# Sixteen row sets change products, three queues change hands, and two gate units change places in a transformer block

## The chip, the cores and the metric

One Trainium2 chip, of which the kernel uses one core. The metric is the device time of one execution in microseconds; the kernel before took 3376.22 us (median of 3 runs, 3374.99 to 3377.64).

A core has five engines with queues of their own: TensorE (PE, with its weight loads as PEld), VectorE (DVE), ScalarE (ACT), GpSimd (POOL) and SyncE (SP). Each works its queue in order. Transfers are issued from the queues of SP, ACT and POOL and share 16 DMA engines.

## The reference, cut to what matters

All tensors are 4-byte floats; there are 512 tokens of width 2048.

```python
h   = rmsnorm(x);  q, k, v, z, gate = split(h @ w_in)
o_a = differential attention of q, k, v (8 heads, chunk mask), normed per head
o_b = spatial gating of gelu(z)
x   = x + (sig(g_A) * (o_a @ P_A) + sig(g_B) * (o_b @ P_B)) @ w_out
# product-key experts ("PEER"), h = rmsnorm(x):
s   = (h @ w_q) against two lists of 128 keys       # 8 heads
16 best of each list, then the 16 best of the 256 sums -> 128 expert numbers and gates a token
a   = h . u_emb[id];  act = gelu(a) * gate;  x = x + sum(act * v_emb[id])
y   = rmsnorm(x) * final_norm
```

## The kernel before

Every dense product is made exact in three passes: a weight tile `raw` is cast to a high half `wh` on ScalarE (L847, L151), VectorE takes the low half `wl = raw - wh` (`split_low`, L111), and TensorE multiplies high by high, high by low and low by high (`mm3`, L162).

The 512 tokens are treated in three ways. The first 128 ("first block") go ahead alone through all layers. Then the other 384 pass attention, gMLP, merge and output product. For the expert layer the tokens split again: 224 tokens, the first block and two extra groups of 64 and 32 (`XG`, each spread over the 128 partitions), are done **sparsely**: GpSimd gathers 128 rows of a table at a time (`indirect_dma_start`, L302), a "set" of 1 MB. A set of `u_emb` costs VectorE one pass that forms a dot product (L281), a set of `v_emb` one pass that adds a scaled row to an accumulator (L288). The remaining 288 tokens (`TD`) are done **densely** over all 16384 experts: the first product (256 steps of 24 matmuls, two steps to a column block `pa`) gives the activations `ga`, stored to `ga_d` by ScalarE's queue (L939); meanwhile a gate matrix is built from one-hots (`gates()`, 72 builds of 4 matmuls `pgt`) and stored to `g_d` in 18 chunks of 16 tokens (L909). The second product (16 groups of 16 steps of 24 matmuls `pvt`) loads `ga` and the gates back (`load_ga`, `load_g`), multiplies them (`gated`, L961), splits the result (`split_gated`) and multiplies it with `v_tiles`; each step's result is added into `accT` by `settle` (L1044).

Sets are spread over the work by a plan. `items` lists them in order: 128 u sets of the first block, its 128 v sets, 96 u sets of the extra groups, their 96 v sets. `knots` gives how many are due at which step (the steps of the first product start at `AT_U` = 240, of the second at `AT_V` = 496), linear between knots; `sparse_step` gathers what is due now and lets VectorE use what was due `GBUF` = 4 steps earlier. 212 are due when the first product starts, and 352 (`U_END`) from 8 steps before the second. The gather waits for a recent `wl` on VectorE (`pace`).

The routing of a 128-token block (`route`) runs on VectorE in portions handed out two steps at a time (`credit`): top 16 lists, then the expert numbers by one-hot sums (L410 to L416), in 4-byte tiles `oh` and `tif`. Block 1 ends by copying numbers and gates into the slots of the extra groups, twelve small transfers on ScalarE's queue (L433, L434).

From L934 on (the first and second product) instructions stand in each queue as written. Ahead of that a scheduler orders them by the program's order and by when tiles come free. `merge` (L724) multiplies a sigmoid of a gate projection (`unit`) with a branch product; its tile pool `gt` (2 buffers) is opened after the attention pools are closed. The last head's norm (`head_norm(att, *tail)`, L716) stands ahead of it.

In the second product `load_g(grp + 2)` is one transfer of 1152 KB on ScalarE's queue at the first step of each group; the first two stand in the last 32 steps of the first product, after the gate matrix is done. At its step 20 the first block's rows are closed (`finish_rows(acc0, ...)`), and each extra group's rows are closed when its last v set is used.

Of the kernel before, what the change touches and what calls it, by code (L numbers as in the profile page):

```python
# [53 lines left out]
def hybrid_block(ctx, tc, x, attn_norm, attn_col, w_in, diff_lambda, diff_subln, gmlp_norm, gmlp_row, wsT, gmlp_bs,  # L54
# [186 lines left out]
    def turned(pair, at, src):  # L241
        for q in range(src.shape[-1] // 512):
# [14 lines left out]
    items = [(table, g, s) for groups in ([-1], range(len(XG))) for table in (u_emb, v_emb)  # L257
             for g in groups for s in range(SLOTS if g < 0 else XSETS[g])]
    U_END = 2 * SLOTS + sum(XSETS)
    AT_U, AT_V = 240, 240 + 2 * NE  # L260
    knots = [(14, 0), (AT_U, 212), (AT_V - 8, U_END), (AT_V, U_END), (AT_V + 222, len(items))]
# [108 lines left out]
    def route(rtp, gbp, tb):  # L370
# [27 lines left out]
        tif = rtp.tile([P, 2 * HEADS, TOPK], F32, name="tif")  # L398
# [5 lines left out]
        for p, rf in enumerate(at):  # L404
            sel = rtp.tile([P, HEADS, TOPK], F32, name=f"sel{p}")
            for hh_ in range(0, HEADS, 2):
                hs = slice(hh_, hh_ + 2)
                oh = rtp.tile([P, 2, TOPK, TOPK], F32, name="oh")
                ohf = oh.rearrange("p h k r -> p (h k) r")
                nc.vector.tensor_tensor(  # L410
                    ohf, rf[:, hs].rearrange("p h k -> p (h k)").unsqueeze(2).to_broadcast([P, 32, TOPK]),
                    iota_f[:, :TOPK].unsqueeze(1).to_broadcast([P, 32, TOPK]), op=OP.is_equal)
                nc.vector.tensor_tensor(
                    oh, oh, tif[:, 2 * hh_ + p:2 * hh_ + 4:2, :].unsqueeze(2).to_broadcast(
                        [P, 2, TOPK, TOPK]), op=OP.mult)
                nc.vector.tensor_reduce(sel[:, hs].rearrange("p h k -> p (h k)"), ohf, axis=AX.X, op=OP.add)  # L416
                yield 1.8
            cols.append(sel.rearrange("p h k -> p (h k)"))
# [6 lines left out]
        if tb == 1:  # L425
# [3 lines left out]
            for g, (t0, n) in enumerate(XG):  # L429
                m = XSETS[g]  # L430
                for j in range(P // n):
                    to, of = slice(j * n, (j + 1) * n), (slice(t0 - P, t0 - P + n), slice(j * m, (j + 1) * m))
                    nc.scalar.dma_start(xslot_e[g][to, :], ei[of])  # L433
                    nc.scalar.dma_start(xslot_g[g][to, :], gf[of])  # L434
# [248 lines left out]
    aa = branch_tiles(0)  # L683
    with tc.tile_pool(name="att", bufs=2, reuse_waits="tile") as att, \
            tc.tile_pool(name="att1", bufs=1, reuse_waits="tile") as att1:
        tail = None
        for h in range(HEADS):
# [27 lines left out]
            tail = (po[:, :LB, :], aa, (slice(None), h))  # L715
        head_norm(att, *tail)  # L716
# [7 lines left out]
    def merge(br, pair):  # L724
        with tc.tile_pool(name="gt", bufs=2, reuse_waits="tile") as gt:
            def unit(n):
                sg = gt.tile([P, LN], F32, name="sg")
                nc.scalar.activation(sg, project(w_in[G0 + KT * br + n], hh, "gate"), AF.Sigmoid)
                return sg

            ahead = [unit(0)]
            for n in range(KT):
                if n + 1 < KT:
                    ahead.append(unit(n + 1))
# [10 lines left out]
    merge(0, aa)  # L745
# [39 lines left out]
    merge(1, bb)  # L785
# [165 lines left out]
    def load_g(grp):  # L951
        if grp < NG:
            gms[grp] = pools["vp"].tile([P, NCH, VG, GCH], F32, name="vg", bufs=2)
            nc.scalar.dma_start(
                gms[grp], g_d[:, :, grp * VG:(grp + 1) * VG, :].rearrange("c p e t -> p c e t"))
# [23 lines left out]
    for i in range(NE):  # L979
        ps = pp_tile("pa")[:, :TD]  # L980
        for half in range(2):
# [17 lines left out]
            if "vp" not in pools and rgen is None and ggen is None:  # L999
# [3 lines left out]
                load_g(0)  # L1003
            elif "vp" in pools:
                u, odd = divmod(step - opened - 2, 2)
# [7 lines left out]
                if u == 5 and not odd:  # L1013
                    load_g(1)
# [8 lines left out]
    with tc.tile_pool(name="pv", bufs=4, space=PSUM, reuse_waits="tile") as pv_pool, \  # L1023
# [89 lines left out]
        for step in range(KT * NG):  # L1113
# [5 lines left out]
            for j in range(VG):  # L1119
# [3 lines left out]
                mm(pv, lo[:, j, :], aH, start=False, stop=j == VG - 1)  # L1123
            if w == 0:
                if n == 0:
                    load_g(grp + 2)
# [17 lines left out]
            if step == 20:  # L1144
# [90 lines left out]
```

## Time and profile before

| | us |
|---|---|
| median of 3 runs | 3376.22 |
| the profiled execution | 3376.36 |
| its span, first to last instruction | 3374.7 |
| TensorE busy | 3245.8 |
| VectorE busy | 2803.2 |
| ScalarE busy | 1561.5 |
| GpSimd busy | 681.0 |

The first product runs from about 1570 to 2518 us of the span, the second from 2518 to 3358. Busy times are sums over the whole span, and its stretches differ; a stretch has to be read by itself. The mean granted clock of TensorE is 0.987 of its full speed. Matmul records overlap, so TensorE counts as busy while its next matmul is already queued.

### The profile page before, as it was taken

To read this page: it belongs to the slowest core of one execution; us is meant where nothing else is said; L and a number is where in the kernel's file an instruction comes from. 1 tells how busy PE (TensorE), PEld (TensorE's weight loads), DVE (VectorE), ACT (ScalarE), POOL (GpSimd) and SP (SyncE) were. 2 spreads that over 40 slices of the span, in tenths; PEclk is the share of its full clock that TensorE was granted. 3 is DMA by queue.
4 is the path that set the end of the run, shared out by engine and by line. 5 is a ranking of instruction groups with operands and counts; after the bars stand their busy time and mean duration, and the time that the engine had idled before them with its cause. 6 is when DMAs were issued, how large, how long until landed. Compare 5 with 4: busy or idle time off the path is not lost. (4 is left out here: it accounts for less than half of the span.)

```text
span 3374.7 us, 53163 instructions
## 1 busy us (share of the span) xinstructions
PE 3245.8 (96%) x20545; PEld 3012.0 (89%) x20545; DVE 2803.2 (83%) x3784; ACT 1561.5 (46%) x2367; POOL 681.0 (20%) x512
## 2 busy tenths in 40 slices
PE   8999999989999999899899999999999999999997
PEld 6577588889989997799899999999999999999997
DVE  7489579888888888899899999777767999989985
ACT  6377234332233332333363588888434343343343
POOL 0000002222322224222223222222321111111100
PEclk9999999999999999899999999999999999999998
DMA  8899847769999999788889999999999999989973
GB/s 321 289 338 349 296 140 253 292 232 357 351 357 339 361 346 411 305 329 315 307 313 365 324 347 355 358 374 358 383 325 350 369 348 359 366 331 363 363 251 131
DMA packets 281101, 1098.47 MB, mean 326 GB/s; under 512 B 28192, under 2 KB 81456, under 8 KB 218320
## 3 DMA queue, kind: packets, MB, share of 16 engines
q1 hardware_dynamic: 152688, 540.74, 43.5%
q0 software_dynamic: 67264, 485.67, 38.4%
q10 hardware_dynamic: 60896, 68.66, 6.0%
q8 instruction: 162, 2.65, 0.3%
q14 instruction: 91, 0.75, 0.1%
HBM read 1047.94 MB, written 46.92 MB: 324 GB/s over the span
## 5 line engine op out<-in xcount | busy, mean ns | idle before, releaser
L111 DVE TENSOR_TENSOR wl<-raw,wh 128x1024 fp32r<-128x1024 f32 x928 | 1128.2, 1222 | 399.8 <-ACT wh L847 234.5
L847 ACT CAST wh<-raw 128x1024 fp32r<-128x1024 f32 x512 | 536.8, 1049 | 811.3 <-PE pvt L1122 301.4
L151 ACT CAST wh<-raw 128x1024 fp32r<-128x1024 f32 x416 | 435.0, 1050 | 679.6 <-PE gate L165 183.5
L166 PE MATMUL pa<-h2H,wl 128*128 128x288 f32 x2048 | 613.8, 300 | 25.4 <-DVE wl L111 24.9
L164 PE MATMUL pa<-h2H,wh 128*128 128x288 f32 x2048 | 613.4, 299 | 19.5 <-ACT wh L847 19.5
L1121 PE MATMUL pvt<-aH,wh 128*128 128x288 f32 x2048 | 609.6, 298 | 0.9 <-ACT wh L847 0.9
L1123 PE MATMUL pvt<-aH,wl 128*128 128x288 f32 x2048 | 605.7, 296 | 3.2 <-DVE wl L111 3.1
L165 PE MATMUL pa<-h2L,wh 128*128 128x288 f32 x2048 | 604.2, 295 | 0.0
L1122 PE MATMUL pvt<-aL,wh 128*128 128x288 f32 x2048 | 602.4, 294 | 0.0
L166 PEld LDWEIGHTS pa<-h2H,wl 128*128 128x128 f32 x2048 | 387.7, 189 | 39.7 <-DVE wl L111 38.7
L164 PEld LDWEIGHTS pa<-h2H,wh 128*128 128x128 f32 x2048 | 388.4, 190 | 20.9 <-ACT wh L847 20.9
L1123 PEld LDWEIGHTS pvt<-aH,wl 128*128 128x128 f32 x2048 | 386.5, 189 | 4.2 <-DVE wl L111 4.1
L165 PEld LDWEIGHTS pa<-h2L,wh 128*128 128x128 f32 x2048 | 388.7, 190 | 0.0
L1121 PEld LDWEIGHTS pvt<-aH,wh 128*128 128x128 f32 x2048 | 386.2, 189 | 2.1 <-ACT wh L847 1.1
L1122 PEld LDWEIGHTS pvt<-aL,wh 128*128 128x128 f32 x2048 | 386.4, 189 | 1.0 <-issue 1.0
L288 DVE SCALAR_TENSOR_TENSOR h2n<-gat,slot_a,h2n 128x2048 f32<-128x2048 f32 x127 | 297.8, 2345 | 4.5 <-DMA gat<-in_v_emb,slot_e 4.5
L302 POOL DMA_INDIRECT gat<-in_v_emb,slot_e x128 | 203.7, 1591 | 478.4 <-DVE wl L111 233.1
L281 DVE SCALAR_TENSOR_TENSOR gat<-gat,h2n 128x2048 f32<-128x2048 f32 x128 | 292.4, 2284 | 0.0
L302 POOL DMA_INDIRECT gat<-in_u_emb,slot_e x128 | 164.2, 1283 | 590.5 <-DVE gat L281 267.9
L302 POOL DMA_INDIRECT gat<-in_u_emb,xslot_e x96 | 162.7, 1695 | 463.3 <-DVE wl L111 455.8
L288 DVE SCALAR_TENSOR_TENSOR accx<-gat,xslot_a,accx 128x2048 f32<-128x2048 f32 x96 | 225.0, 2344 | 3.4 <-DMA gat<-in_v_emb,xslot_e 3.4
L302 POOL DMA_INDIRECT gat<-in_v_emb,xslot_e x96 | 105.0, 1094 | 598.3 <-DVE wl L111 590.3
(424 smaller groups left out, 5930.1 us busy)
## 6 DMA issues: line engine op xcount, KB each, us to landing
raw<-in_uT SPq DMA_DIRECT2D x256, 512.0 KB, 7.9
raw<-in_v_tiles SPq DMA_DIRECT2D x256, 512.0 KB, 7.2
raw<-in_e_nat SPq DMA_DIRECT2D x144, 512.0 KB, 5.2
raw<-in_w_nat SPq DMA_DIRECT2D x128, 512.0 KB, 6.1
raw<-in_w_in SPq DMA_DIRECT2D x112, 512.0 KB, 6.6
ga_d<-ga ACTq DMA_DIRECT2D x128, 144.0 KB, 6.8
g_d<-gs ACTq DMA_DIRECT2D x18, 1024.0 KB, 11.5
vg<-g_d ACTq DMA_DIRECT2D x16, 1152.0 KB, 24.8
```

Of the source, the lines that this page charges most:

```text
L111: return nc.vector.tensor_tensor(low, full, high.bitcast(F32), op=OP.subtract)
L151: nc.scalar.copy(hi, raw)
L164: mm(ps, hi[:, k, :], xh[:, k0 + k, c0:c1], start=first and k == 0, stop=False)
L165: mm(ps, hi[:, k, :], xl[:, k0 + k, c0:c1], start=False, stop=False)
L166: got = mm(ps, lo[:, k, :], xh[:, k0 + k, c0:c1], start=False, stop=last and k == 7)
L281: used = nc.vector.scalar_tensor_tensor(row, row, 1.0, h2n if g < 0 else h2x[g], op0=OP.mult, op1=OP.mult, accum_out=a)
L288: used = nc.vector.scalar_tensor_tensor(acc, row, a, acc, op0=OP.mult, op1=OP.add)
L302: got = nc.gpsimd.indirect_dma_start(out=row, out_offset=None, in_=items[i][0], in_offset=bass.IndirectOffsetOnAxis(ap=column(i, slot_e, x ...
L847: nc.scalar.copy(hi, src)
L1121: mm(pv, hi[:, j, :], aH, start=j == 0, stop=False)
L1122: mm(pv, hi[:, j, :], aL, start=False, stop=False)
L1123: mm(pv, lo[:, j, :], aH, start=False, stop=j == VG - 1)
```

## The change

The plan takes 112 of the first block's v sets ahead of the extra groups' u sets and 16 behind them, in the second product; its last knot moves from 222 to 238 steps into that product, and the first block's rows are closed at its step 44 instead of 20. The twelve slot copies are issued by GpSimd. `load_g` is issued by GpSimd in six parts of three chunks, one a step; the uses of the first group's gates move back by six steps. `tif` and `oh` become 2-byte tiles. The pool `gt` has three buffers and is opened ahead of the attention pools, and two gate units stand ahead of the last head's norm.

```diff
-    items = [(table, g, s) for groups in ([-1], range(len(XG))) for table in (u_emb, v_emb)
-             for g in groups for s in range(SLOTS if g < 0 else XSETS[g])]
-    U_END = 2 * SLOTS + sum(XSETS)
+    EARLY_V = 112
+    items = [(u_emb, -1, s) for s in range(SLOTS)] + [(v_emb, -1, s) for s in range(EARLY_V)]
+    items += [(u_emb, g, s) for g in range(len(XG)) for s in range(XSETS[g])]
+    U_END = len(items)
+    items += [(v_emb, -1, s) for s in range(EARLY_V, SLOTS)]
+    items += [(v_emb, g, s) for g in range(len(XG)) for s in range(XSETS[g])]
-    knots = [(14, 0), (AT_U, 212), (AT_V - 8, U_END), (AT_V, U_END), (AT_V + 222, len(items))]
+    knots = [(14, 0), (AT_U, 212), (AT_V - 8, U_END), (AT_V, U_END), (AT_V + 238, len(items))]
...
-        tif = rtp.tile([P, 2 * HEADS, TOPK], F32, name="tif")
+        tif = rtp.tile([P, 2 * HEADS, TOPK], BF16, name="tif")
...
-                oh = rtp.tile([P, 2, TOPK, TOPK], F32, name="oh")
+                oh = rtp.tile([P, 2, TOPK, TOPK], BF16, name="oh")
...
-                    nc.scalar.dma_start(xslot_e[g][to, :], ei[of])
-                    nc.scalar.dma_start(xslot_g[g][to, :], gf[of])
+                    nc.gpsimd.dma_start(xslot_e[g][to, :], ei[of])
+                    nc.gpsimd.dma_start(xslot_g[g][to, :], gf[of])
...
+    gt = branch.enter_context(tc.tile_pool(name="gt", bufs=3, reuse_waits="tile"))
+    def unit(gt, br, n):
+        sg = gt.tile([P, LN], F32, name="sg")
+        nc.scalar.activation(sg, project(w_in[G0 + KT * br + n], hh, "gate"), AF.Sigmoid)
+        return sg
...
+        ahead = [unit(gt, 0, n) for n in range(2)]
         head_norm(att, *tail)
...
-    def load_g(grp):
+    def load_g(grp, part):
         if grp < NG:
-            gms[grp] = pools["vp"].tile([P, NCH, VG, GCH], F32, name="vg", bufs=2)
-            nc.scalar.dma_start(
-                gms[grp], g_d[:, :, grp * VG:(grp + 1) * VG, :].rearrange("c p e t -> p c e t"))
+            if part == 0:
+                gms[grp] = pools["vp"].tile([P, NCH, VG, GCH], F32, name="vg", bufs=2)
+            c = slice(part * GPART, part * GPART + GPART)
+            nc.gpsimd.dma_start(
+                gms[grp][:, c], g_d[c, :, grp * VG:(grp + 1) * VG, :].rearrange("c p e t -> p c e t"))
...
-                u, odd = divmod(step - opened - 2, 2)
+                part = step - opened
+                if part < NCH // GPART:
+                    load_g(0, part)
+                elif part < 2 * (NCH // GPART):
+                    load_g(1, part - NCH // GPART)
+                u, odd = divmod(step - opened - 8, 2)
...
+            if n < NCH // GPART:
+                load_g(grp + 2, n)
             if w == 0:
-                if n == 0:
-                    load_g(grp + 2)
                 gated(u + 4)
...
-            if step == 20:
+            if step == 44:
                 ends.append(finish_rows(acc0, 0, P, add_first))
```

## Rows read from the trace of the kernel before

**Rows 1.** Busy times of the page: engine, us (share of the span), instructions.
```profile
PE 3245.8 (96%) x20545; PEld 3012.0 (89%) x20545; DVE 2803.2 (83%) x3784; ACT 1561.5 (46%) x2367; POOL 681.0 (20%) x512
```

**Rows 2.** Stretch, us, then PE, PEld, DVE, ACT, POOL busy, clock, DMA share, GB/s.
```profile
2728.40:2957.20 228.80, 228.80 (x1731) 228.80 (x1730) 207.87 (x248) 87.79 (x108) 30.85 (x31) 1.00 0.97 361
```

**Rows 3.** By stretch, first product: tile pa alone, then everything.
```profile
2196.70:2254.50 57.80, 52.63 (x385) 50.97 (x385) 3.21 (x8) 1.00 0.95 364
...
2196.70:2254.50 57.80, 57.80 (x451) 57.80 (x449) 42.82 (x43) 50.46 (x97) 13.16 (x9) 1.00 0.95 364
```

**Rows 4.** By stretch, everything, first product's other stretches.
```profile
1648.50:1717.90 69.40, 57.36 (x404) 55.50 (x404) 55.77 (x94) 28.93 (x51) 19.82 (x10) 0.90 0.79 282
1717.90:1811.80 93.90, 85.56 (x628) 82.09 (x627) 87.49 (x185) 54.06 (x89) 25.63 (x17) 1.00 0.93 337
1811.80:1892.40 80.60, 78.58 (x581) 76.70 (x580) 78.31 (x92) 29.58 (x40) 27.10 (x14) 1.00 0.96 361
1892.40:1988.30 95.90, 88.88 (x667) 86.22 (x665) 93.70 (x235) 69.96 (x133) 23.32 (x18) 1.00 0.92 322
1988.30:2078.90 90.60, 88.12 (x674) 86.90 (x673) 83.15 (x108) 78.59 (x148) 25.53 (x14) 1.00 0.94 344
2397.40:2518.00 120.60, 108.79 (x769) 106.81 (x769) 83.30 (x85) 41.90 (x57) 31.03 (x16) 0.94 0.97 361
```

**Rows 5.** Order of time, ScalarE, around 1677: start, duration, engine, line, idle before.
```profile
1677.33 1.04 ACT L847 CAST wh<-raw 128x1024 fp32r<-128x1024 f32 x1 [16.82 <-DMA xslot_g<-gate]
```

**Rows 6.** Order of time, ScalarE and its queue, then TensorE, 2402 to 2468.
```profile
2402.66 2.08 ACT L847 CAST wh<-raw 128x1024 fp32r<-128x1024 f32 x2 [7.71 <-DMA g_d<-gs]
...
2405.07 7.83 ACTq L939 DMA_DIRECT2D ga_d<-ga  x1
...
2466.19 1.04 ACT L847 CAST wh<-raw 128x1024 fp32r<-128x1024 f32 x1 [10.15 <-DMA vg<-g_d]
...
2467.28 0.61 PE L164 MATMUL pa<-h2H,wh 128*128 128x288 f32 x1 [4.61 <-ACT wh L847]
```

**Rows 7.** Groups by line, VectorE: busy, mean ns, idle before.
```profile
L288 DVE SCALAR_TENSOR_TENSOR accx<-gat,xslot_a,accx 128x2048 f32<-128x2048 f32 x96 | 225.0, 2344 | 3.4 <-DMA gat<-in_v_emb,xslot_e 3.4
```

**Rows 8.** Groups by line, GpSimd, whole span; then gathers 1570 to 2078, 2626 to 3294.
```profile
L380 POOL DMA_DIRECT2D score<-h2x_d x6 | 3.2, 544 | 0.0
...
L302 POOL DMA_INDIRECT gat<-in_v_emb,slot_e x45 | 94.4, 2098 | 210.5 <-DVE wl L111 193.2 <-DVE cv L320 11.3 <-DVE ef L421 5.4
...
L302 POOL DMA_INDIRECT gat<-in_v_emb,xslot_e x84 | 88.4, 1053 | 521.1 <-DVE wl L111 513.4 <-issue 7.6 <-DVE nrt L1081 0.2
```

**Rows 9.** The page's GB/s in 40 slices of the span.
```profile
GB/s 321 289 338 349 296 140 253 292 232 357 351 357 339 361 346 411 305 329 315 307 313 365 324 347 355 358 374 358 383 325 350 369 348 359 366 331 363 363 251 131
```

**Rows 10.** TensorE's wait, ScalarE's sigmoid, then tile gate by stretch.
```profile
731.51 0.88 PE L210 MATMUL pt<-ident,o 128*128 128x128 f32 x3 [4.38 <-DVE o L498]
...
733.61 1.28 ACT L728 ACT_TABLE_LOAD   x1
734.90 0.49 ACT L728 ACTIVATE sg<-gate 128x384 f32<-128x384 f32 x1
...
694.00:718.40 24.40, 19.42 (x96) 16.37 (x96) 0.00 (x0) 0.00 (x0) 1.00 0.62 219
735.30:745.90 10.60, 10.46 (x48) 10.18 (x48) 0.00 (x0) 0.47 (x2) 0.80 0.50 167
750.00:758.60 8.60, 8.60 (x48) 8.33 (x48) 0.00 (x0) 0.00 (x0) 1.00 0.92 345
```

**Rows 11.** Groups by line, VectorE: the one-hot product.
```profile
L413 DVE TENSOR_TENSOR oh<-oh,tif 128x512 f32<-128x512 f32 x32 | 22.1, 690 | 1.0
```

**Rows 12.** By stretch, everything: 208 steps of the second product.
```profile
2626.20:3294.40 668.20, 668.05 (x5011) 663.90 (x5010) 598.68 (x724) 261.70 (x324) 92.71 (x86) 1.00 0.92 342
```

**Rows 13.** Order of time, TensorE: an output turn's wait.
```profile
3316.88 0.50 PE L1052 MATMUL yps<-ident,accT 128*32 128x128 f32 x3 [1.92 <-DVE accT L1044]
```

**Rows 14.** Transfers: median us from issue to landing.
```profile
gat<-in_v_emb,xslot_e POOLq DMA_INDIRECT x96, 9.2
```

More of the change, by code (lines that the diff above doesn't have):

```diff
@@ L722, in hybrid_block, with merge @@
     mT = mgp.tile([P, KT, LN], F32, name="mT")
[L724 to L731, printed above, removed]
+    def merge(br, pair, gt, ahead):
+        if True:
             for n in range(KT):
-                if n + 1 < KT:
-                    ahead.append(unit(n + 1))
+                if n + 1 < KT and n + 1 >= len(ahead):
+                    ahead.append(unit(gt, br, n + 1))
                 sg = ahead[n]
@@ L743, in merge @@
                     nc.vector.tensor_add(mT[:, n, :], mT[:, n, :], sg)
-    merge(0, aa)
+    merge(0, aa, gt, ahead)
     branch.close()
@@ L784, in hybrid_block @@
             split_pair(bb, (slice(None), g), obf)
-    merge(1, bb)
+    gt = branch.enter_context(tc.tile_pool(name="gt", bufs=3, reuse_waits="tile"))
+    merge(1, bb, gt, [unit(gt, 1, 0)])
     branch.close()
@@ L949, in load_ga @@
             nc.sync.dma_start(gas[u], ga_d[u])
-    def load_g(grp):
+    GPART = 3
+    def load_g(grp, part):
         if grp < NG:
-            gms[grp] = pools["vp"].tile([P, NCH, VG, GCH], F32, name="vg", bufs=2)
-            nc.scalar.dma_start(
-                gms[grp], g_d[:, :, grp * VG:(grp + 1) * VG, :].rearrange("c p e t -> p c e t"))
+            if part == 0:
[3 more added lines that the diff above has]
+                gms[grp][:, c], g_d[c, :, grp * VG:(grp + 1) * VG, :].rearrange("c p e t -> p c e t"))
     def gated(u):
@@ L1002, in hybrid_block @@
                 opened = step
-                load_g(0)
+                load_g(0, 0)
             elif "vp" in pools:
-                u, odd = divmod(step - opened - 2, 2)
+                part = step - opened
[4 more added lines that the diff above has]
+                u, odd = divmod(step - opened - 8, 2)
                 if 0 <= u < 4 and not odd:
@@ L1012, in hybrid_block @@
                     load_ga(u)
-                if u == 5 and not odd:
-                    load_g(1)
         before = i, ps
@@ L1143, in hybrid_block @@
                 nc.scalar.dma_start(fgain, bcast_rows(final_norm, D))
-            if step == 20:
+            if step == 44:
+                assert eaten[0] >= U_END + SLOTS - EARLY_V, eaten
                 ends.append(finish_rows(acc0, 0, P, add_first))
```

## The prediction

> **What bounds the kernel now.** I read the page's busy times first [rows 1]: TensorE is busy 96% of the span, VectorE 83%, ScalarE 46%, GpSimd 20%. So the time is the matmul stream plus the places where that stream runs dry, and a change that leaves the matmuls alone can only win those places back. To find them I took the busy times by stretch, cut at step starts. An undisturbed stretch gives the price of a step: 72 steps of the second product (24 matmuls each, hence about 1728 records) take 228.8 us, 3.178 us a step [rows 2]. Where the gate matrix is built beside the first product, 16 steps take 57.8 us; less 16 x 3.178 = 50.85 this leaves 6.95 us for 8 builds (4 matmuls, 8 records each), 0.87 us a build [rows 3].
>
> Now each stretch of the first product against its floor (steps x 3.178 + builds x 0.87; the builds are the records beyond 24 a step, divided by 8) [rows 4]:
> - from 1648.5, 16 steps and 2 builds: floor 52.6, took 69.4, lost 16.8; VectorE busy 55.8
> - from 1717.9, 24 steps and 6 builds: floor 81.5, took 93.9, lost 12.4; VectorE 87.5
> - from 1811.8, 24 steps: floor 76.3, took 80.6, lost 4.3; VectorE 78.3
> - from 1892.4, 24 steps and 11 builds: floor 85.8, took 95.9, lost 10.1; VectorE 93.7
> - from 1988.3, 24 steps and 12 builds: floor 86.7, took 90.6, lost 3.9; VectorE 83.2
> - from 2397.4, 32 steps: floor 101.7, took 120.6, lost 18.9; VectorE 83.3
>
> Two kinds of loss stand side by side. In the second to fifth stretch VectorE's own work is above or near TensorE's floor: there VectorE is the bound. In the first and the last VectorE has room, and ScalarE's queue is what stops. Around 1670 ScalarE stands 16.82 us without a weight cast, issuing the twelve slot copies and waiting around them [rows 5]. In the last stretch it waits 7.71 us for the gate write in front of its load, is held 7.83 us in the next store behind that load, and later waits 10.15 us behind the second load; TensorE's wait of 4.61 us for a cast is the trace of it [rows 6]. The granted clock of 0.90 and 0.94 in just these two stretches says that matmuls behind the gaps also ran at the lower of its two levels, 1.2 GHz instead of 2.4 [rows 4].
>
> **The change part by part.** The sum is made against the profiled execution, 3376.36 us (span 3374.7 and 1.66 around it), 0.14 above the median of 3376.22.
>
> *Sixteen sets moved.* A set costs VectorE 2.344 us [rows 7]. The first product held 140 sets in 248 steps (352 less the 212 due by its start), now 124: 0.0645 a step fewer, 0.151 us of VectorE a step, 3.6 us in 24 steps. VectorE's work becomes 53.4, 83.9, 74.7, 90.1 and 79.6 us in the five stretches before 2078.9. Each can end no earlier than the larger of this and the floor: 53.4, 83.9, 76.3, 90.1, 86.7. I allow each a little above, since routing work comes in bursts; the second 3 us, since its loss (12.4) was twice what VectorE's excess over the floor (6.0) explains.
>
> *Slot copies to GpSimd's queue.* ScalarE's 16.82 us go. What is late next is VectorE, 53.4 against the floor of 52.6. On GpSimd twelve issues at 0.544 us, the price of a plain issue there [rows 8], make 6.5 us behind the wait for the slot numbers; the next row gathers queue behind them. Gathers are issued 4 steps (12.7 us) ahead of their use, which covers most. I end this stretch at 55.4: gain 14 (bounds 8, if the gathers come 6.5 us late, and 16). The others, with the moved sets: 7, 3.5, 5.5 and 2, together 18 (bounds 9, half of it, and 25.4, the whole excess over the larger term).
>
> *Gate loads to GpSimd, in six parts.* Each part waits only for its three chunks, so the wait for the last gate write falls on part six, and ScalarE's casts no longer stand behind any. What remains are the transfers. The stretch moved 361 GB/s x 120.6 us = 43.5 MB; less 1.6 sets of 1.05 MB it is 41.8 MB, and in 101.7 us that would need 411 GB/s, as much as the best slice of the page shows and above all others [rows 9]. At 383, the next best slice, 109 us. I take 108.6: gain 12 (bounds 8, at 371 GB/s, and 18.9).
>
> No row shows a plain GpSimd transfer in 512-byte pieces: 3 chunks x 128 partitions make 384 pieces a part. Whole plain issues cost 0.544 us whatever their rows; a gather of 128 pieces 1.053 us in the second product, 2.098 in the VectorE-bound first [rows 8]. So a part lies between 0.54 and 6.3 us (three times 2.098). I take three times the nearest row, the plain issue: 1.6 us, 10 us a group of 16 steps (50.8 us), beside 7.5 gathers at 1.053, 8 us. GpSimd is then busy a third of the time and nothing waits for it.
>
> The Trainium skill (SBUF — State Buffer, section "SBUF: two separate sides") says that descriptors of GpSimd's own queue are written by GpSimd, which VectorE's two-port operations lock out, and advises the hardware queues instead; this speaks against the move. The trace agrees so far as gathers cost twice as much where VectorE is full (2.098 against 1.053 us); by that rule the parts would be slow, and it is the second rival below.
>
> *Merge gates ahead.* TensorE waits 4.38 us for the last head's norm, and the next gate unit runs 10.6 us instead of 8.6 at a granted clock of 0.80 [rows 10]. Two units' matmuls (96) already stood ahead of it, between 694 and 718.4, but their sigmoid runs only at 734.90, after the head's last work: their tiles' pool opens when the attention pools are done. With a pool of their own and a third buffer, the sigmoids free PSUM early and a third unit, 8.6 us of matmuls, can stand in the gap. I take 6 of 4.38 + 2.0 (bounds 8.6, and -2.6: the sigmoid's table load of 1.28 us twice among the last head's exponentials).
>
> *Two-byte one-hots.* 0.69 us each, 24 in the first product [rows 11]. The nearest row is the same operation at four bytes, so I take no gain (bounds 0 and 16.6 us of VectorE); any gain falls in stretches that the moved sets already bring to TensorE's floor.
>
> *The second product.* VectorE was busy 598.7 of 668.2 us [rows 12]. Sixteen sets add 37.5, the first block's two closing passes, moved in from step 20, 4.7: 640.9, 96%. TensorE hides this as long as its three split weights ahead cover the bursts; I take +2. At the end, sets stop at step 242 instead of 226, so the last group's closing pass (2.35 us) meets the output turns, where TensorE already waits 1.92 us for VectorE [rows 13]: +3. The stalls of the first block's close leave steps 16 to 32: -2. Sum +3 (bounds -3 and +40, all the vector work on the path).
>
> Total: 14 + 18 + 12 + 6 - 3 = 47; 3376.36 - 47 = 3329.
>
> **The rivals.**
> *The second product gives it back.* If the 96% of VectorE doesn't hide, the path takes up to 37.5 us more: 3329 + 37.5 = 3367, half of it 3348. For it: bursts beside settling and splitting. Against it: in the 228.8 us at 91% TensorE never starved [rows 2, 12].
> *GpSimd becomes the bound (slower).* With p the price of 128 pieces, a group costs GpSimd (6 x 3 + 7.5) x p = 25.5 p against 50.8 us. It binds above p = 1.99, and eats the whole 47 us over 13 groups above p = 2.13; at the 2.098 us of the first product it costs 2.7 x 13 = 35 (3364), at 2.4 us 10.4 x 13 = 135, that is 3464. For it: the doubled gather price where VectorE is full, which the second product now is. Against it: 1.053 us there so far, at 90%, and plain issues at a quarter of it [rows 8].
> *Moved requests come late.* GpSimd's waits and issues delay the rows, VectorE stands, and half of the first product's 44 us stay: 3351. For it: a gather lands 9.2 us after its issue, of the 12.7 us of lead [rows 14]. Against it: ScalarE's stall had delayed them more.
>
> **How the numbers follow.** My forecast has 0.66, 3329 with a range of its own of 3312 to 3345; the second product gives back 0.11; late requests 0.10; GpSimd the bound 0.08; more than all this (the whole losses won, below 3308) 0.05. From 3308 to 3360 about 0.17 is left out: the 0.05 below, 0.08 for GpSimd, and part of the first rival. Within 0.2% (6.8 us, what a measurement can tell from no change) needs 40 us given back and more: 0.04, the tail of the first rival and the mildest of the second. Slower: 0.08, GpSimd and what joins it. Faster: 0.88.
>
> **What would show it.** Right: ScalarE without waits of 7 us and more on slot copies and gate loads; the stretch of the slot copies near 55 us for 16 steps; the last 32 steps near 109; a gate unit between the last head's scores and its norm; 208 steps of the second product near 670 us with VectorE at 96%. Wrong: GpSimd parts above 2 us; VectorE waiting for rows; TensorE waiting for low halves all through the second product; a total above 3360.

## The result and the profile after

The changed kernel takes 3320.51 us (median of 4 runs, 3313.51 to 3328.04) against 3375.6 (4 runs, 3372.68 to 3377.64): ratio 0.9839, 95% interval 0.9823 to 0.9854. The forecast was 3329, with a range of 3308 to 3360. The profiled execution took 3313.51 us (span 3311.8), 7.0 below the median, so its stretches add up to more than the medians show: 62.9 us against 55.1.

Cut at the same steps as [rows 2 to 4], spans of the two profiled executions:

| stretch | before | after | change | forecast |
|---|---|---|---|---|
| start to the first query matmul | 432.6 | 431.0 | -1.6 | |
| to the first gate matmul | 261.7 | 267.7 | +6.0 | |
| to the end of the first merge (first `pn` matmul) | 225.2 | 212.6 | -12.6 | -6, with the line above |
| to the first product | 650.6 | 650.4 | -0.2 | |
| its steps 0 to 24 | 78.4 | 76.7 | -1.7 | 0 |
| steps 24 to 40 (slot copies) | 69.4 | 54.1 | -15.3 | -14 |
| steps 40 to 136 | 361.1 | 342.3 | -18.8 | -18 |
| steps 136 to 224 | 318.4 | 315.8 | -2.6 | 0 |
| steps 224 to 256 (gate loads) | 120.7 | 104.3 | -16.4 | -12 |
| second product, steps 0 to 32 | 108.2 | 101.7 | -6.5 | |
| steps 32 to 240 | 668.2 | 666.6 | -1.6 | +3, the three |
| step 240 to the end | 80.3 | 88.7 | +8.4 | |

The page after, to be read beside [rows 1]:

```profile
PE 3221.1 (97%) x20545; PEld 2996.5 (90%) x20545; DVE 2791.3 (84%) x3784; ACT 1565.5 (47%) x2369; POOL 882.1 (27%) x620
vg<-g_d POOLq DMA_DIRECT2D x96, 192.0 KB, 9.5
```

VectorE's and ScalarE's work is what it was; GpSimd has 201 us more and is still idle for three quarters of the time. The same stretches as in [rows 4], and the 208 steps of [rows 12] (columns: us, then PE, PEld, DVE, ACT, POOL busy, clock, DMA share, GB/s):

```profile
1638.40:1692.50 54.10, 53.55 (x404) 52.80 (x403) 50.78 (x92) 29.01 (x51) 25.17 (x21) 1.00 0.92 331
1692.50:1779.70 87.20, 84.48 (x627) 81.91 (x626) 83.93 (x184) 54.00 (x89) 37.05 (x15) 1.00 0.94 346
1779.70:1855.90 76.20, 76.20 (x582) 76.20 (x581) 73.00 (x101) 29.58 (x40) 32.32 (x13) 1.00 0.98 362
1855.90:1946.80 90.90, 88.66 (x667) 86.27 (x665) 88.69 (x231) 71.02 (x135) 33.47 (x16) 1.00 0.92 319
1946.80:2034.70 87.90, 87.54 (x674) 86.79 (x673) 80.92 (x108) 79.40 (x150) 34.89 (x13) 1.00 0.94 347
2350.60:2454.90 104.30, 102.55 (x771) 101.50 (x770) 77.02 (x78) 41.55 (x56) 44.76 (x24) 1.00 0.98 379
2556.60:3223.10 666.50, 664.97 (x5001) 662.14 (x5001) 625.04 (x736) 261.30 (x320) 171.99 (x171) 1.00 0.97 366
```

The granted clock is 1.00 in all of them; 0.90 and 0.94 are gone. The third stretch stands at its floor of 76.3 (floors as in the prediction: TensorE's own work in the stretch), the fifth 1.2 above 86.7; the second (87.2 against 83.9 of VectorE and 81.5 of TensorE) and the fourth (90.9 against 88.7 and 85.8) are still VectorE's. In the last row VectorE is busy 94%, and TensorE waits only 1.5 us for its low halves in all of the 666.5 us.

ScalarE and GpSimd where the slot copies are (start, duration, engine, line, idle before):

```profile
1664.09 1.05 ACT L853 CAST wh<-raw 128x1024 fp32r<-128x1024 f32 x1 [2.12 <-PE pa L165]
1667.26 1.05 ACT L853 CAST wh<-raw 128x1024 fp32r<-128x1024 f32 x1 [1.82 <-PE pa L165]
```
```profile
1653.06 0.58 POOL L436 DMA_DIRECT2D xslot_e<-ei  x1 [1.08 <-DVE ei L430]
...
1660.55 0.50 POOL L437 DMA_DIRECT2D xslot_g<-gate  x1
1661.35 2.62 POOL L305 DMA_INDIRECT gat<-in_v_emb,slot_e  x1 [0.30 <-issue]
```

The casts wait for TensorE alone; the 16.82 us of [rows 5] are gone. The twelve issues take 8 us of GpSimd, 1.8 of them in two waits, the next gather stands behind them, and its rows come in time: VectorE waits for none in this stretch.

In the last 32 steps TensorE waits 1.7 us in all:

```profile
PE pa L166 <- DVE wl L111: 1.3, 2, 0.7
PE pa L164 <- ACT wh L853: 0.4, 1, 0.4
```

The merge: the first two sigmoids now run among the last head's exponentials, each with its table load, and TensorE has no wait above 0.2 us between 690 and 750. Before, it stood 8.6 us in the stretch of the merge (the 4.38 of [rows 10] and waits of 2.0, 1.3, 0.7 and 0.2), and its clock was 0.89 and 0.91 from 694 to 760. The first two rows are before, the third after (columns as above), then ScalarE after:

```profile
694.30:735.30 41.00, 32.53 (x188) 28.12 (x187) 32.58 (x60) 14.56 (x29) 12.36 (x11) 0.89 0.69 255
735.30:760.00 24.70, 24.56 (x129) 24.56 (x130) 18.61 (x18) 7.44 (x10) 4.79 (x5) 0.91 0.69 246
698.70:735.00 36.30, 36.11 (x222) 33.37 (x222) 32.10 (x56) 17.96 (x31) 9.07 (x8) 1.00 0.71 260
```

```profile
712.95 1.28 ACT L691 ACT_TABLE_LOAD   x1
714.24 0.49 ACT L691 ACTIVATE sg<-gate 128x384 f32<-128x384 f32 x1
...
719.65 1.28 ACT L474 ACT_TABLE_LOAD   x1
...
722.49 1.28 ACT L691 ACT_TABLE_LOAD   x1
723.78 0.49 ACT L691 ACTIVATE sg<-gate 128x384 f32<-128x384 f32 x1
```

Two losses are new. At 468 us, in the value projection of the first head, TensorE waits for a low half, and VectorE shows why: between the split at 453.62 and the next at 466.65 stand only the one-hots of the first block's routing (rows: TensorE, then VectorE's splits and the routing's last two operations). Behind the wait the clock is 0.54 for 3.6 us.

```profile
467.93 0.51 PE L190 MATMUL pv<-wl,hH 128*128 128x512 f32 x1 [3.75 <-DVE wl L111]
```
```profile
453.62 1.21 DVE L111 TENSOR_TENSOR wl<-raw,wh 128x1024 fp32r<-128x1024 f32 x1
466.19 0.29 DVE L424 SCALAR_TENSOR_TENSOR ef<-sel,sel 128x128 f32<-128x128 f32 x1
466.51 0.23 DVE L426 CAST slot_e<-ef 128x128 int32<-128x128 f32 x1
466.65 3.49 DVE L111 TENSOR_TENSOR wl<-raw,wh 128x1024 fp32r<-128x1024 f32 x3
```

And at the end an output turn (`yps`, which transposes finished results on TensorE) waits 4.90 us where it waited 1.92 [rows 13], because the last group's closing pass (L1098) meets the output's own work on VectorE. Of the 8.4 us more in this stretch some 3.4 are moved, not lost: the closing of the last extra group stood in steps 224 to 232 before and took that much there.

```profile
3270.55 0.78 PE L1065 MATMUL yps<-ident,accT 128*32 128x128 f32 x3 [4.90 <-DVE accT L1057]
```
```profile
3262.29 1.87 DVE L1071 TENSOR_TENSOR gat<-gat,yps 32x512 f32<-32x512 f32 x3 [1.09 <-PE yps L1065]
3264.09 1.88 DVE L1079 TENSOR_TENSOR gat<-gat,fgain 32x512 f32<-32x512 f32 x3
...
3266.65 2.35 DVE L1098 SCALAR_TENSOR_TENSOR gat<-accx,nry,fgain 128x2048 f32<-128x2048 f32 x1
```

### The profile page after: what moved, and what is told of

Its sections match the earlier page's. It is cut to its first block, busy times and chain, and to the rows that moved or that the text cites. A ratio compares the mean times of both kernels' runs of the same rounds, so it can differ in the third digit from the quotient of the medians.

```text
span 3311.8 us, 53252 instructions
## 1 busy us (share of the span) xinstructions
PE 3221.1 (97%) x20545; PEld 2996.5 (90%) x20545; DVE 2791.3 (84%) x3784; ACT 1565.5 (47%) x2369; POOL 882.1 (27%) x620
## 3 DMA queue, kind: packets, MB, share of 16 engines
q0 software_dynamic: 73792, 504.65, 41.1%
## 5 line engine op out<-in xcount | busy, mean ns | idle before, releaser
L305 POOL DMA_INDIRECT gat<-in_u_emb,xslot_e x96 | 263.2, 2741 | 397.7 <-DVE wl L111 389.7
L305 POOL DMA_INDIRECT gat<-in_v_emb,slot_e x128 | 211.2, 1650 | 462.2 <-DVE wl L111 233.3
L305 POOL DMA_INDIRECT gat<-in_u_emb,slot_e x128 | 171.9, 1343 | 578.7 <-DVE gat L284 247.7
```

The costliest lines, as they stand in the source:

```text
L305: got = nc.gpsimd.indirect_dma_start(out=row, out_offset=None, in_=items[i][0], in_offset=bass.IndirectOffsetOnAxis(ap=column(i, slot_e, x ...
```

## The experiments

Stretches are of the profiled executions; where a whole time is compared with the changed kernel's, that is by the ratios to the kernel before, since they ran on different chips.

### Each part alone, in the kernel before

These four ran together: 3375.18 us for the kernel before (20 runs).

**Slot copies alone.**
```diff
-                    nc.scalar.dma_start(xslot_e[g][to, :], ei[of])
-                    nc.scalar.dma_start(xslot_g[g][to, :], gf[of])
+                    nc.gpsimd.dma_start(xslot_e[g][to, :], ei[of])
+                    nc.gpsimd.dma_start(xslot_g[g][to, :], gf[of])
```


> The kernel before, with the twelve slot copies alone issued by GpSimd. The sum's theory (each stall is paid where it stands): the 16 steps of that stretch go from 69.4 to about 57 us, VectorE's unreduced work of 55.8 us being the floor now; total about 12 us less, 3364. Rival (the vector work is the bound there and the stall was hidden under it): the wait moves to VectorE and the rows behind GpSimd's queue come late; at most 4 us less, 3372.

3358.01 us, ratio 0.9947 (0.9928 to 0.9967): 17 us. Steps 24 to 40 went from 69.4 to 59.1; with the moved sets as well they come to 54.1. Only 10.3 of the 17 us stand there: the last 32 steps of the first product took 3.6 less and the first 32 of the second 5.1 less, which this edit does not touch, and no run tells why.

**Gate loads alone**, in parts on GpSimd, with the uses of the first group six steps later.
```diff
-            nc.scalar.dma_start(
-                gms[grp], g_d[:, :, grp * VG:(grp + 1) * VG, :].rearrange("c p e t -> p c e t"))
+            nc.gpsimd.dma_start(
+                gms[grp][:, c], g_d[c, :, grp * VG:(grp + 1) * VG, :].rearrange("c p e t -> p c e t"))
```


> The kernel before, with the gate loads alone moved: GpSimd's queue, six parts. Sum's theory: the last 32 steps of the first product go from 120.6 to about 106 us, nothing else moves; total 12 to 16 us less, 3360 to 3364. Rival (the transfers are at their limit there, so another queue wins nothing): at most 5 us less, 3371. Rival (GpSimd becomes the bound in the second product): slower there, above 3376.

3363.26 us, ratio 0.9966 (0.9954 to 0.9977): 12 us. The last 32 steps went from 120.7 to 109.4, near what the forecast had for them (108.6).

**Merge alone.**
```diff
+    gt = branch.enter_context(tc.tile_pool(name="gt", bufs=3, reuse_waits="tile"))
...
+        ahead = [unit(gt, 0, n) for n in range(2)]
         head_norm(att, *tail)
```


> The kernel before, with the two gate units ahead of the last head's norm and the pool of three buffers alone. If the gap around 731 us is filled by a third gate unit: first product starts 8 to 13 us earlier, total 3363 to 3368. Rival (the sigmoid's table loads among the last exponentials eat it): within 3 us of before.

3370.69 us, ratio 0.9984 (0.9971 to 0.9997): 4.5 us, less than expected. Around the merge 12.8 us are won (225.2 to 212.4), as much as in the whole change, and 8.5 lost ahead of it (261.7 to 270.2): the early loss comes with this part, not with the one-hots. (The profiled execution is the longest of the ten, 3378.93; what it has too much stands elsewhere, 5.3 us in the first product and 3.5 in the second.) The edit does three things, the two units ahead of the norm, the pool's earlier place and its third buffer; no run takes them apart.

**Moved sets alone**, with the first block's rows closed at step 44.
```diff
-    knots = [(14, 0), (AT_U, 212), (AT_V - 8, U_END), (AT_V, U_END), (AT_V + 222, len(items))]
+    EARLY_V = 112
+    items = [(u_emb, -1, s) for s in range(SLOTS)] + [(v_emb, -1, s) for s in range(EARLY_V)]
...
+    knots = [(14, 0), (AT_U, 212), (AT_V - 8, U_END), (AT_V, U_END), (AT_V + 238, len(items))]
```


> The kernel before, with the sixteen sets alone moved (last knot 238, closing at step 44). Sum's theory: the VectorE-bound stretches of the first product lose 15 to 20 us, both ScalarE stalls stay (about 17 and 19 us), the second product costs 0 to 5 more; total 12 to 20 us less, 3356 to 3364. Rival (the second product gives the sets back): within 5 us of before, or slower. Rival (the sets explain all of the gain): 40 us less and more, 3335 or below.

3347.63 us, ratio 0.992 (0.9895 to 0.9944): 27.5 us, the largest part, and more than expected. Beside steps 40 to 136 (361.1 to 344.7) they also eased steps 24 to 40 by 5.3 and the last 32 by 8.4, where the forecast counted other parts. The four sum to 61 us, the whole change to 55: parts overlap in the last 32 steps (11.3 and 8.4 alone, 16.4 together).

### Gate loads: the pieces or the queue

**One transfer a group, on GpSimd.**
```diff
-    GPART = 3
+    GPART = 18
...
-                elif part < 2 * (NCH // GPART):
-                    load_g(1, part - NCH // GPART)
+                elif part == 6:
+                    load_g(1, 0)
```


> The changed kernel with each gate load as one transfer again, on GpSimd's queue; the first still at the first step after the gate matrix, the second six steps later, the uses as late as in the change. Theory (ScalarE's queue was the whole trouble, the pieces add little): GpSimd now stands about 7 us for the last gate write, and the gathers behind it have 12.7 us of lead; the last 32 steps of the first product go from 104.3 us to 104 to 108, and the whole is 3320 to 3326 us. Rival (the pieces matter, because a gather stuck behind a whole load comes late): the 32 steps go back to 112 or more, and the 13 loads of the second product cost some us too: 3330 us or more.

3329.53 us, ratio 0.9865 (0.9845 to 0.9885); on the same chip as the next run, 10 us more. Neither theory: the last 32 steps stay at 104.9, since the wait for the gate write is only 0.8 us here; the loss is in the second product, whose time above TensorE's floor (256 steps at 3.178 us, the price from [rows 2]) goes from 28.2 to 39.0 us. There VectorE waits 5.6 us for rows and TensorE 6.8 for low halves (changed kernel: 0.7 and 1.5). Issue and landing of the loads, first of this kernel, then of the changed one (rows: count, ns min/median/max; us to landing, min/median/max):

```profile
L964 POOL DMA_DIRECT2D vg<-g_d x16: 1273/1277/1300, 2359.1 to 3140.9; - x16
...
DMA to landing us min/median/max: 11.9/14.2/16.9
```
```profile
L964 POOL DMA_DIRECT2D vg<-g_d x96: 738/790/843, 2349.6 to 3135.7; - x96
...
DMA to landing us min/median/max: 5.4/9.5/13.1
```

GpSimd spends less on the whole load (1.3 us a group) than on six parts (4.7), so its time is not what costs. The moved sets alone, with whole loads on ScalarE's queue, show nearly half of it (33.2 us above the floor, TensorE waiting 5.1 for low halves). 1152 KB at once between gathers and weights is the likely cause; no run changed that alone.

**The six parts on ScalarE's queue.**
```diff
-            nc.gpsimd.dma_start(
+            nc.scalar.dma_start(
                 gms[grp][:, c], g_d[c, :, grp * VG:(grp + 1) * VG, :].rearrange("c p e t -> p c e t"))
```


> The changed kernel with the six parts of each gate load on ScalarE's queue instead of GpSimd's. Theory (the queue is what matters): the sixth part waits on ScalarE for the last gate write, as the whole load did before, and gate casts and splits stand behind it; the last 32 steps of the first product go from 104.3 us to 110 to 117, the whole is 3326 to 3335 us, and ScalarE shows an idle time of 5 us or more in front of a cast behind a gate write. Rival (six pieces are enough, whatever the queue): 3320 to 3324 us and no such wait.

3319.58 us, ratio 0.9836 (0.9816 to 0.9856): as fast as the change, and the rival is right about the time. A wait like the one that the theory named is there too, though: ScalarE stands once for 7.79 us, with a held store in front as in [rows 6]:

```profile
2369.44 2.15 ACTq L945 DMA_DIRECT2D ga_d<-ga  x1
2376.71 0.37 ACTq L964 DMA_DIRECT2D vg<-g_d  x1
2377.19 1.04 ACT L853 CAST wh<-raw 128x1024 fp32r<-128x1024 f32 x1 [7.79 <-DMA raw<-in_uT]
```

It costs TensorE 2.1 us, and the 32 steps take 107.2 instead of 104.3. Steps 40 to 136 and the tail took 2.7 and 2.4 us more, the tail in the run before this one too (91.2 us). Held 7.83 us behind a whole load, the store is held 2.15 behind parts. In these 32 steps, then, six parts on either queue keep the gain to within 3 us, and so does a whole load on GpSimd's queue. What the three have in common is the later first use (and the moved sets), and no run has the later use alone: how much of the gain it is stays open. Over the whole kernel parts are as good on either queue.

### One-hots

```diff
-        tif = rtp.tile([P, 2 * HEADS, TOPK], BF16, name="tif")
+        tif = rtp.tile([P, 2 * HEADS, TOPK], F32, name="tif")
...
-                oh = rtp.tile([P, 2, TOPK, TOPK], BF16, name="oh")
+                oh = rtp.tile([P, 2, TOPK, TOPK], F32, name="oh")
```


> The changed kernel with the one-hots (oh, tif) in 4 bytes again. The product of one 128x512 one-hot then takes 0.69 us instead of 0.43; 24 of them stand in the first product, 6.3 us of VectorE, and VectorE is busy 172.6 of the 178.1 us of the two routing stretches there. Theory of the prediction (these stretches are already near TensorE's floor, so nothing comes of it): the two stretches stay within 1 us of 87.2 and 90.9, the whole is 3318 to 3323 us. Rival (VectorE is still the bound while it routes): the two stretches take 2 to 3 us more each, 3324 to 3327 us.

3325.47 us, ratio 0.9857 (0.9836 to 0.9878): in the rival's range, but by the intervals not to be told from the change. The two stretches stayed at 87.2 and 90.9, but the expectation had put the one-hots there wrongly: by their start times none stands there, and VectorE's busy time is the same in both kernels (172.8 and 172.6). The 24 stand in steps 12 to 27, 66 to 81 and 123 to 137, and there next to nothing came of them: steps 0 to 24 take 76.7 us in both kernels, 64 to 88 76.8 against 76.2, 112 to 136 87.4 against 88.0. Steps 24 to 40 take 57.9 instead of 54.1, but only two of the one-hots stand there (0.5 us); what is new is that VectorE waits for a gathered row (us in total, times, longest), which it does not in the changed kernel:

```profile
DVE h2n L291 <- DMA gat<-in_v_emb,slot_e: 3.7, 1, 3.7
```

The last run below has 5.4 us of such waits there and takes 56.7: behind the slot copies rows do come late in some kernels, as the prediction's third rival has it, and no run tells why in these. The early wait grows from 3.8 to 5.7 us, near the 2.1 us that eight longer one-hots add to the chain in front of the split. So the 2 bytes are worth about 2 us behind the early loss, and nothing that shows in the first product.

### The early loss

```diff
-            ef = rtp.tile([P, SLOTS], F32, name="ef")
+            ef = rtp.tile([P, SLOTS], F32, tag="down", name="ef")
```


> The changed kernel with one line more: the expert numbers ef of the routing share the tile of down, which makes the routing's pool 512 bytes a partition smaller. In the changed kernel the gates' pool of 4.5 KB pushes the attention pools up, so that the first head's q lies over the routing tiles of the first block; its copy then stands two casts later, and three of the splits of pv's weights stand behind all one-hots of that routing instead of among them. With the 512 bytes q is clear of them and the old order is back. Theory (this order is the early loss of the change): the wait of TensorE of 3.75 us at 464 us goes, the stretch from the first query matmul to the first gate matmul goes from 267.7 to 261.7 us, and the whole is 3313 to 3316 us. Rival (the early loss has another cause, as the load queue): the stretch stays at 266 or more and the whole at 3319 to 3322 us.

3315.14 us, ratio 0.9831 (0.9811 to 0.9851), which alone can't be told from the change. The stretch went from 267.7 to 261.9, as the theory said, and TensorE's wait is gone. It takes 267.2 to 270.5 us in all six kernels here that have the early pool without this line, and 260.8 to 262.0 in the eight others. VectorE's splits stand among the one-hots again:

```profile
453.11 1.22 DVE L111 TENSOR_TENSOR wl<-raw,wh 128x1024 fp32r<-128x1024 f32 x1
457.21 1.22 DVE L111 TENSOR_TENSOR wl<-raw,wh 128x1024 fp32r<-128x1024 f32 x1
461.58 1.22 DVE L111 TENSOR_TENSOR wl<-raw,wh 128x1024 fp32r<-128x1024 f32 x1
465.68 1.22 DVE L111 TENSOR_TENSOR wl<-raw,wh 128x1024 fp32r<-128x1024 f32 x1
468.71 0.29 DVE L424 SCALAR_TENSOR_TENSOR ef<-sel,sel 128x128 f32<-128x128 f32 x1
```

So the early loss comes with the early pool and goes with this line. That it is a matter of addresses (a tile that lies over another's memory must wait for it, and the scheduler orders everything around that wait) is the expectation's account and fits; but addresses stand in no row, and the line also ties `ef` to `down`'s tile, so this part is argued, not shown.

### Where the sets end, and how many move

**Last knot at 226, in the changed kernel.**
```diff
-    knots = [(14, 0), (AT_U, 212), (AT_V - 8, U_END), (AT_V, U_END), (AT_V + 238, len(items))]
+    knots = [(14, 0), (AT_U, 212), (AT_V - 8, U_END), (AT_V, U_END), (AT_V + 226, len(items))]
```


> The changed kernel with the last knot of the plan at step 226 of the second product instead of 238. The sets end 12 steps earlier, so VectorE has the last group's closing pass behind it before the output turns; 5 more sets (12 us of VectorE) stand in steps 32 to 240, where VectorE was busy 625 of 666.5 us. Theory (the tail loss of 8.4 us is the meeting of sets and closing pass with the output turns): the stretch from step 240 to the end goes from 88.7 to 81 to 84 us, the middle stays within 3 us, the whole is 3313 to 3318 us. Rival (VectorE at 96% in the middle gives it back): the middle takes 6 us or more longer, 3320 us or more.

3317.26 us, ratio 0.9828 (0.9806 to 0.9851). The tail is won (88.7 to 80.0) and the middle gives it back (666.6 to 673.9), as the rival has it; its reason is not shown, though. By groups of 8 steps, the time above the floor stands in a few places, 3.4 us where an extra group's rows are closed and the rest around the first block's close and the output turns; between them the groups are at the floor. The sum over the 256 steps is 27.7 us before, 28.2 after, 26.9 here. Of the middle's 7.3 us, 3.4 are the last group's closing, which moved across step 240; some 4 more stand in steps 24 to 64, around the first block's close (6.3 above the floor against 2.0), and why is open.

**Last knot at 232**, with the smaller routing pool.
```diff
-    knots = [(14, 0), (AT_U, 212), (AT_V - 8, U_END), (AT_V, U_END), (AT_V + 238, len(items))]
+    knots = [(14, 0), (AT_U, 212), (AT_V - 8, U_END), (AT_V, U_END), (AT_V + 232, len(items))]
```


> The changed kernel with the smaller routing pool and the last knot at step 232, half way between 226 and 238; 16 sets moved as in the change. Theory (what knot 226 wins at the tail, VectorE gives back in the middle, nearly one for one): the middle takes 669 to 672 us, the tail 83 to 86, and the whole stays within 2 us of 3315. Rival (the tail is won as soon as the closing pass stands ahead of the output turns, and the middle pays only for the last steps): tail 80 to 82, middle 666 to 668, 3307 to 3311 us.

3311.15 us, the lowest median of all, ratio 0.9818 (0.9794 to 0.9841); by its interval it can't be told from the change. Middle 673.1 (expected 669 to 672), tail 80.7 (83 to 86), above the floor 27.6: the same sum once more, with the same two pieces (3.0 in steps 232 to 240, and 6.1 in steps 24 to 64).

**Eight sets moved instead of sixteen**, smaller routing pool, knot 226.
```diff
-    EARLY_V = 112
+    EARLY_V = 120
...
-    knots = [(14, 0), (AT_U, 212), (AT_V - 8, U_END), (AT_V, U_END), (AT_V + 238, len(items))]
+    knots = [(14, 0), (AT_U, 212), (AT_V - 8, U_END), (AT_V, U_END), (AT_V + 226, len(items))]
```


> The changed kernel with the smaller routing pool (ef in down's tile), 8 sets moved instead of 16 (EARLY_V 120) and the last knot at step 226 instead of 238. Theory (VectorE's own work sets steps 32 to 240 of the second product above about 0.47 sets a step, and the sets that meet the output turns set the tail): the middle stays at 662 to 668 us since its sets fall to 0.46 a step, the tail is 80 to 82 us, and the 8 sets that go back cost the routing stretches of the first product 3 to 5 us together; the whole is 3307 to 3313 us. Rival (each set costs its 2.344 us wherever it stands): 18.8 us come back in the first product for 8.7 won at the tail, 3320 us or more.

3323.84 us, ratio 0.985 (0.9828 to 0.9872): a miss. The first product takes 14.8 us more than with 16 sets moved and the same pool (910.2 against 895.4), 1.85 us a set. The other kernels built on the change with 16 sets took 892.1 to 898.9 there, so the price is 11 to 18 us, or 1.4 to 2.3 a set; the second has 18.8 us less of VectorE's work and is no faster (27.3 above the floor, against 27.8). Most of a set's 2.344 us was on the path where it stood, and none where it went. The fourth and the sixth stretch of the table above, here:

```profile
1856.00:1951.10 95.10, 90.23 (x667) 87.80 (x665) 92.79 (x238) 69.72 (x133) 27.74 (x17) 0.98 0.89 316
...
2359.60:2467.50 107.90, 104.67 (x771) 103.32 (x770) 80.19 (x81) 41.48 (x56) 41.30 (x24) 0.98 0.99 380
```

The first is VectorE's excess (92.8 against 88.7). In the second VectorE has room; what is up is the traffic, 107.9 us x 380 GB/s = 41.0 MB against 39.5, at the same rate.

**Twenty-two sets moved**, smaller routing pool, knot 238.
```diff
-    EARLY_V = 112
+    EARLY_V = 106
...
-            if step == 44:
+            if step == 52:
```


> The changed kernel with the smaller routing pool, 22 sets moved instead of 16 (EARLY_V 106) and the first block's rows closed at step 52 instead of 44; last knot 238 as in the change. In the second product 8 sets more or fewer, or a knot at 226, 232 or 238, left the sum of all groups of 8 steps above TensorE's floor at 27 to 28 us, while 8 sets taken back into the first product cost 14.8 us there. Theory (a set costs time only in the first product, as long as VectorE in the second stays below its span): the 6 sets more win 5 to 9 us in the first product, steps 32 to 240 stay within 3 us of 666, with VectorE busy near 639 of it, and the whole is 3305 to 3311 us. Rival (VectorE at 96% has no room left for its bursts): the second product takes 5 us or more longer and the whole stays at 3314 us or more.

3318.38 us, ratio 0.9838 (0.9825 to 0.9852): also a miss. The first product stays (896.4 against 895.4), and the second takes 34.0 us above the floor instead of 27.8, with VectorE at 95% in steps 32 to 240:

```profile
2556.00:3227.50 671.50, 667.71 (x5003) 664.06 (x5002) 638.23 (x742) 261.11 (x320) 168.73 (x178) 1.00 0.98 373
```

Of those 6.2 us, 4.9 stand in steps 48 to 96 (6.9 above the floor against 2.0), behind the first block's close. That was moved too, and the three runs above have 5.5 to 5.9 in steps 48 to 64 with no more sets; so the six sets are not shown to cost it. Eight moved sets are too few: each that stays costs its time in the first product. Past 16 nothing more is won there, and the whole times (0.9831 and 0.9838) do not tell 16 from 22.

## Why the prediction was right, and where not

**Slot copies** (14 forecast, 15.3 found). The mechanism held, with two causes in one stretch: alone they leave 59.1, and the moved sets take it from there to 54.1. GpSimd's twelve issues took 8 us, of which 1.8 were two waits; 6.5 were forecast. In the changed kernel no row came late for it; in two of the kernels above some did, for 3.7 and 5.4 us.

**The other VectorE-bound stretches** (18 forecast, 18.8 found). The larger of VectorE's work and TensorE's floor was the right bound: forecast ends of 86.9, 77.1, 90.4 and 88.6, found 87.2, 76.2, 90.9 and 87.9. That the sum fits to 1 us is in part luck: steps 40 to 136 took 342.2 to 349.1 us in the kernels above with 16 sets moved. (The upper bound given for this term, 25.4, is 24.0 by its own rows.) Not forecast were 4.3 us less in steps 0 to 24 and 136 to 224. The moved sets alone have both (76.7 and 315.9); but the second stretch takes 315.8 with the gate loads alone too, so its 2.6 us are not the sets' for certain.

**Gate loads** (12 forecast, 16.4 found). The size came out larger because the moved sets alone give 8.4 there; the transfer bound that held the forecast back was too high, for the stretch moved 379 GB/s x 104.3 us = 39.5 MB, not 41.8. The reason was partly wrong: the forecast put the gain down to ScalarE's queue, and the parts on that same queue kept all but 3 us of it.

**The price of a part** (1.6 us, with 0.54 to 6.3 as bounds) was 0.79. The rival in which GpSimd becomes the bound needed 1.99 for each 128 pieces, three times that for a part; a group of 16 steps costs GpSimd 6 x 0.79 + 7.5 x 1.118 = 13 us of 51. The Trainium skill (SBUF — State Buffer, "SBUF: two separate sides") says that GpSimd cannot write descriptors while VectorE runs an operation in a two-port mode, and advises the hardware queues. With VectorE busy 94% the parts kept to 738 to 843 ns, and parts on ScalarE's queue gave the same time: nothing of the kind hit these transfers. No row tells which of VectorE's operations here hold both ports, so the rule itself was not tested; the prediction took it that enough of them do.

**Merge** (6 forecast, 6.6 found): right by luck, since two errors cancel. The stretch of the merge gave 12.6, above the bound of 8.6. The forecast had counted the longest wait and one slow gate unit, 4.38 + 2.0. In fact TensorE stood 8.6 us in that stretch and stands 0.3 now, and its own work, now at the full clock, takes 4.3 us less (212.3 against 216.6). The early loss took 6.0 of it back, and the forecast did not have it, since it read a pool that opens earlier as free. The run with the smaller routing pool shows that stretch without the 6 us; its whole time does not stand clear of the change's.

**One-hots** (0 forecast): the product fell from 0.69 to 0.43 us. In the first product nothing of it showed, as forecast, since the one-hots stand where TensorE is at its floor; about 2 us of it shorten the early loss, which the forecast did not have. The nearest row, the same operation at four bytes, was a poor guide. The Trainium skill (VectorE: DVE Perf Modes, "Mode 2×_1P — pack two bf16 into one 32-bit read") says that operands of two bytes go two at a time; here the product with all operands in 2 bytes gained, and the comparison, whose inputs stay at 4 bytes, kept its 0.69 us.

**Second product** (+3 forecast, +0.3 found). The parts of the sum were nearly as put (the first block's close leaves steps 16 to 32: 6.5 us less there, 2.0 more in steps 48 to 64, -2 forecast; the tail +8.4 instead of +3), and the main claim held: at 94% VectorE is hidden. The 96% were not put to the test: of the sixteen sets only twelve more fall in these 208 steps (98 instead of 86), so VectorE is busy 625.0 us of them, where the forecast had 640.9. With six sets more, at 95%, the second product took 6.2 us more; whether that is the first rival or the later close is open.

The median is 8.5 us below the forecast. Against the profiled execution the sum is 15.9 us short: 4.4 in the gate loads' stretch, 4.3 in the two stretches held to be at their floor, 2.7 in the second product, 1.6 at the start (which took 430.9 to 436.4 us in the kernels above, whatever they changed), the rest in small terms of 1.3 and less.

## What to carry to other kernels

Where two engines are near their limits in one stage and one of them has room in another, moving work paid nearly its full price here until the first stage was at the other engine's floor, and nothing beyond: work out both floors stretch by stretch and move just so much. A load's queue, its pieces and the time of its first use are three changes: try each on its own, since here pieces on the old queue did as well as on the new one. A pool that opens earlier can cost time far from the change (here 6 us, 230 us ahead of it); read the stretch ahead of the change too. And one profiled execution is no exact price: steps 40 to 136 of the same plan took 342.2 us in one and 349.1 in another.

## What the runs showed of the hardware

A plain transfer's issue on GpSimd grows little with its pieces: 0.50 to 0.59 us for a slot copy, 0.79 us for 384 pieces of 512 bytes (as the kernel's access has them), 1.28 us for 2304, with VectorE above 90% busy. The same 1152 KB land 14.2 us after the issue from GpSimd's queue and 24.8 us after it from ScalarE's in the kernel before (medians); VectorE waited for late rows in the second product with both, 5.6 and 3.4 us.

The two queues also cut the same bytes differently. ScalarE's queue on the page, before and after (packets, MB, share):

```profile
q10 hardware_dynamic: 60896, 68.66, 6.0%
q10 hardware_dynamic: 23072, 49.69, 4.0%
```

The gate loads and slot copies took 37824 packets and 19.0 MB with them; GpSimd's queue has the same 19.0 MB more, but only 6528 packets more (67264 to 73792). By the trace's packet sizes the gate loads are 36864 packets of 512 bytes on ScalarE's queue, and GpSimd's has 4608 more of 4096 bytes, the same bytes. So on GpSimd's queue eight pieces go as one packet; whether that is why they land sooner, no run shows.

A gather's record takes 2.74 us in the first product of the changed kernel (the extra groups' `u_emb`) and 1.12 us in the second, though VectorE is busy 94% in the second and only 74% in the last 32 steps of the first, where they take as long (2.80); so VectorE's load, by which the prediction read the gathers' price, doesn't explain it, and no run tells what does.
